# A two-layer hybrid decoder trunk on one core: earlier cache pages, 230 GB/s assumed for transfers, a hand-ordered second MLP and four branch steps moved to ScalarE

## The chip, the cores and the metric

The kernel runs on one core of one Trainium2 chip. The metric is the device time of one execution in microseconds (us). Engines are named as in the profile: PE is TensorE's matmul, PEld its weight load, DVE is VectorE, ACT is ScalarE, POOL is GpSimd, SP is SyncE, which here issues the DMA transfers.

## The reference, cut to what matters

Two layers, width 1024, over 1024 prompt rows and 8 samples of 4 rows each (1056 rows in all). Float32 throughout.

```python
# even layer: attention of 8 heads of 64 beside a recurrent branch of width 512
q, k, v, xr, g = jnp.split(u @ w_in, [512, 1024, 1536, 2048], axis=-1)
attn = _stick_breaking(q, concat(past_k, k), concat(past_v, v), sb_bias, q_offset)
xc   = bias + sum(w[j] * xp[:, j:j + t] for j in range(4))        # causal conv of xr
r, i = sigmoid(xc @ wa + ba), sigmoid(xc @ wx + bx)               # 8 blocks of 64
a    = exp(-8 * softplus(-lam) * r)
inp  = sqrt(-expm1(2 * log_a)) * (i * xc)
h    = scan(h = a * h + inp)
out  = concat(attn, gelu(g) * h) @ w_out
# odd layer: 16 heads, three dilated windows (128,1), (512,4), (2048,16), merged by their denominators
# behind each mixer:
h = h + square(relu(rms_norm(h) @ w_ff1)) @ w_ff2                 # 1024 -> 4096 -> 1024
```

For the samples, `past_k` and `past_v` are gathered from a pool of pages by a page table: 8 samples with 8 pages of 128 keys, so 64 pages of keys and 64 of values, 256 KB each.

## The kernel before, in words

**Matmuls.** Activations lie transposed, features on partitions and the 1056 rows in three pieces of 352 columns (`CW`). Float32 operands are split into a high and a low part, and a product is three matmuls (`mm3`). A raw weight tile `ws` is split by ScalarE, which copies the high part (two instructions of 128x512), and GpSimd, which subtracts it for the low part (one of 128x1024). One weight unit (128x1024) feeds 72 matmuls of 352 columns.

**Order of the work.** Two kinds of stretches follow each other. In most of them the tile framework's scheduler orders each engine. In the attention stretches and in the first MLP the order is written by the program: generators of attention steps, projections and sample steps are merged by `interleave`, and a small planner (`Clock`, L60, and `Timed`, L128) keeps for each engine and tile the time at which it expects it to be free. Deferred steps (`after`, L263, a delay in columns of 1/2.4 ns) come up when their time has passed. A transfer costs the planner its bytes at 360 GB/s (L143). Cache pages and other work tiles come from a ring of 18 tiles `u` and are handed back by `drop`; the planner picks the one that it expects free first.

**Stages of the even layer.**
- The recurrent branch: four blocks of 128 features. PE projects `xr` and `g`, DVE takes them out of PSUM (`xr<-mm,rstd`, `g<-mm,rstd`). `lru_conv` (L638) makes `xc` (a scaled copy of `xr`, then three shifted multiply-adds). `lru_block` (L658) makes the GELU factor `ge`, the gates `u` and `ig` (PE matmuls, ScalarE sigmoids), `a` and `z` by ScalarE's exp, tanh and reciprocal root, then on DVE `w = u + 1`, `e = (a+1)*w`, `e = 0.25*e - 1`, `e = (a+1)*e` and so on to the scan `hsc`. GpSimd multiplies `ge` and `ig`.
- Attention of four pairs of heads: `heads` and `projections` interleaved. The first three pairs run before the sample stage; the fourth is interleaved with it. Results go to DRAM (`mix<-o`) and come back transposed (`x<-mix`).
- The sample stage `sb_samples` (L1436): a generator that first asks for four pages (`fetch`), splits and places the queries, then takes 64 key pages and 64 value pages, four of them in flight, and asks for the next as each is used. It is created behind the loop over the pairs. Beside it runs `early_out`, the half of the output projection that the branch feeds.

**MLPs.** `finish_layer` (L1213) makes the output projection and norm, then the MLP: 8 groups of 4 up units (`w1`, 128 hidden features each) and 4 down units (`w2`, 256 outputs each). For layer 0 `first_mlp` (L1264) writes the order of all five engines by hand: the raw weight of unit `u+4` is asked for and that of unit `u+2` is cut in two halves between the pieces of unit `u`. For layer 1 a plain loop asks for each unit's weights in place and the scheduler orders it; the last four down units come from `last_weights`, and `last_pass` (L1367) does the last group together with the final norm, transposes and stores.

In the loop of layer 1 a hidden piece takes this path (L1242 to L1250):

```python
nc.vector.scalar_tensor_tensor(t, ps, 0.0, rstd[:, s], op0=OP.max, op1=OP.mult)
nc.scalar.activation(q, t, AF.Square)
nc.scalar.activation(th[f][:, s], q, AF.Copy)
nc.vector.tensor_sub(tl[f][:, s], q, f32(th[f][:, s]))
```

and a down unit adds its product to `h` on DVE (`h<-mm,h`). Up and down products share two PSUM tiles `mm`.

Of the kernel before, what the change touches and what calls it, by code (L numbers as in the profile page):

```python
# [11 lines left out]
F = mybir.dt.float32  # L12
# [24 lines left out]
def f32(ap):  # L37
    return ap.bitcast(F)
# [89 lines left out]
class Timed:  # L128
# [5 lines left out]
    def __getattr__(self, n):  # L134
        f = getattr(self.engine, n)

        def call(*args, **kw):
            r = f(*args, **kw)  # L138
            aps = [a for a in list(args) + list(kw.values()) if hasattr(a, "name") and hasattr(a, "shape")]
            outs = aps[:1] + ([kw["accum_out"]] if "accum_out" in kw else [])  # L140
            if self.e == "sync":
                o = aps[0] if aps[0].space != DRAM else aps[1]
                cost = int(np.prod(o.shape)) * 4 / 360 * 2.4  # L143
                outs = [a for a in outs if a.space != DRAM]
                ins = [a for a in aps[1:] if a.space != DRAM]
            else:
                a, b = Timed.NS[self.e]
                ins = aps[1:]
                c = int(np.prod(aps[0].shape[1:]))
                if self.e == "vector" and c >= 256:  # L150
                    big = [i for i in ins if i.space != PSUM and int(np.prod(i.shape[1:])) == c]
                    b *= 2 if "scan" in n else 1.6 if len(big) > 1 else 1
                cost = (a + b * c + (130 if "accum_out" in kw else 0)) * 2.4
            self.clock.run(self.e, cost, outs, ins)
            return r
        call.timed = True
        return call
# [18 lines left out]
class Trunk:  # L176
# [152 lines left out]
        self.nc.sync.dma_start(s, src)  # L329
        return s  # L330

    def parts_w(self, kb, cols, pool=None, bufs=4):
        return [(pool or self.wp).tile([128, kb, cols], R, name=self.nm("w"), tag="w", bufs=bufs) for _ in range(2)]

    def split_w(self, s, h, l):
        kb = h.shape[1]
# [301 lines left out]
    def lru_conv(self, f, xr, oc, T):  # L638
        nc = self.nc
        V = self.vec[:, f]  # L640
        cw = [V[:, 32 + j:33 + j] for j in range(4)]
        xrs = xr[:, SEQ:].rearrange("p (b t) -> p b t", t=4)
        xc = T("xc")
        nc.vector.tensor_scalar(xc, xr, cw[3], V[:, 36:37], op0=OP.mult, op1=OP.add)
        xp = T("xp", shape=(128, 8, 7))
        nc.gpsimd.tensor_copy(xp[:, :, 0:3], V[:, 0:24].rearrange("p (b j) -> p b j", j=3))
        nc.gpsimd.tensor_copy(xp[:, :, 3:7], xrs)
        xcs = xc[:, SEQ:].rearrange("p (b t) -> p b t", t=4)
        for j in (2, 1, 0):
            d = 3 - j  # L650
            nc.vector.scalar_tensor_tensor(xc[:, d:SEQ], xr[:, :SEQ - d], cw[j], xc[:, d:SEQ],
                                           op0=OP.mult, op1=OP.add)
            nc.vector.scalar_tensor_tensor(xcs, xp[:, :, j:j + 4], cw[j], xcs, op0=OP.mult, op1=OP.add)
        nc.gpsimd.tensor_copy(oc[:, f, 0:3], xr[:, SEQ - 3:SEQ])
        nc.gpsimd.tensor_copy(oc[:, f, 3:27].rearrange("p (b j) -> p b j", j=3), xrs[:, :, 1:4])
        return xc

    def lru_block(self, f, g, xc, bd, sp4, tiny, oc, T):  # L658
# [2 lines left out]

        ge = T("ge")
        nc.scalar.activation(ge, g, AF.Square)
        nc.vector.tensor_scalar(ge, ge, 0.044715, 1.0, op0=OP.mult, op1=OP.add)
        nc.gpsimd.tensor_mul(ge, ge, g)
        u, ig = T("u"), T("ig")
        for dst, m, bc in ((u, bd[f], 37), (ig, bd[4 + f], 38)):
# [11 lines left out]
        nc.scalar.activation(u, u, AF.Tanh, scale=sp4[:, 0, f:f + 1])  # L679
        nc.scalar.activation(z, u, AF.Abs_reciprocal_sqrt, bias=tiny)  # L680
        w, e = T("w"), T("e")
        nc.vector.tensor_scalar_add(w, u, 1.0)
        nc.vector.scalar_tensor_tensor(e, a, 1.0, w, op0=OP.add, op1=OP.mult)
        nc.vector.tensor_scalar(e, e, 0.25, -1.0, op0=OP.mult, op1=OP.add)
        nc.vector.scalar_tensor_tensor(e, a, 1.0, e, op0=OP.add, op1=OP.mult)
        nc.vector.tensor_mul(a, u, e)
        nc.scalar.activation(a, a, AF.Identity, scale=2.0, bias=1.0)
# [321 lines left out]
    def layer0(self, st, rstd):  # L1009
# [4 lines left out]
        with self.pool("smp0") as sp, self.pool("qkv0") as qkv:  # L1014
            def TS(tag, bufs=1, dtype=F, shape=(128, NT)):
                return sp.tile(list(shape), dtype, name=self.nm(tag), tag=tag, bufs=bufs)
# [5 lines left out]
            with self.pool("pair0") as pool:  # L1022
# [52 lines left out]
                def load_lru(k):  # L1075
# [5 lines left out]
                att = self.heads(pps, lambda p, pp, h, i: self.sb_scores(pp, T, h, 2 * p + h, i),  # L1081
                                 k_step, v_step, T, False, done, 2)
                proj = self.projections(st, rstd, win, 512, pps, T)
                self.low_queries(T)
                with self.manual():
                    self.interleave((proj, 1))
                    for p in range(4):
                        self.split_pair(pps[p], T, False)
                        if p == 0:
                            self.after(60000, self.states_out, oc, TS("ot", shape=(36, LRU)), need=[oc])  # L1090
                        if p < 3:
                            self.interleave((att, 106.6 if p else 85.8), (proj, 76))
                    sample = self.sb_samples(smp, pps[3], ats, T, x, load, lambda: first.append(
                        self.out_w(self.i["w_out_ab"][0], range(4), 0, 9000)))
                    early = self.early_out(0, self.i["w_out_ab"][0], ops, range(4, 8),
                                           load_lru, lambda k: True, ("q32", "k32"), pps[3], T)
                    self.interleave((att, 126), (sample, 340), (early, 95))
# [115 lines left out]
    def finish_layer(self, l, ops, wsrc, ks, w):  # L1213
# [7 lines left out]
        with self.pool(f"mlp{l}") as hp:  # L1221
# [7 lines left out]
            w1 = self.i["w_ff1"][l].rearrange("(k p) f -> p k f", p=128)  # L1229
            w2 = self.i["w_ff2"][l].rearrange("(f p) d -> p f d", p=128)  # L1230
            nx = {}
            if l == 0:
                self.first_mlp(st, rstd, w1, w2, h, nx)
                return nx
            for g in range(8):
                th = [hp.tile([128, NT], R, name=self.nm("th"), tag="th", bufs=6) for _ in range(4)]
                tl = [hp.tile([128, NT], R, name=self.nm("tl"), tag="tl", bufs=6) for _ in range(4)]
                for f in range(4):
                    c0 = (g * 4 + f) * 128
                    w = self.weights(w1[:, :, c0:c0 + 128], 8, 128)  # L1240
                    if g == 7 and f == 3:
                        last = self.last_weights(w2)  # L1242

                    def ev(ps, s, f=f):
                        t = hp.tile([128, CW], F, name=self.nm("t"), tag="t", bufs=3)
                        q = hp.tile([128, CW], F, name=self.nm("t2"), tag="t2", bufs=3)
                        nc.vector.scalar_tensor_tensor(t, ps, 0.0, rstd[:, s], op0=OP.max, op1=OP.mult)
                        nc.scalar.activation(q, t, AF.Square)
                        nc.scalar.activation(th[f][:, s], q, AF.Copy)
                        nc.vector.tensor_sub(tl[f][:, s], q, f32(th[f][:, s]))  # L1250
                    for _ in self.project(st, w, ev):
                        pass
                if g == 7:
                    self.last_pass(last, th, tl, h)
                    break
                for m2 in range(4):
                    w = self.weights(w2[:, g * 4:g * 4 + 4, m2 * 256:(m2 + 1) * 256], 4, 256)
                    for _ in self.contract(w, (2 * m2, 2 * m2 + 1), range(4), th, tl, h):
                        pass
        return nx  # L1260

    def first_mlp(self, st, rstd, w1, w2, h, nx):  # L1264
        nc, hp = self.nc, self.hp
        todo = self.caches(hp)
        raw, parts = {}, {}

        def load(u):
# [7 lines left out]
        def cut(u, half):  # L1277
            if u >= 64:
                return
            if half == 0:  # L1280
                parts[u] = self.parts_w(*raw[u].shape[1:], *((hp, 2) if u % 3 == 2 else ()))
            (a, b), kb = parts[u], raw[u].shape[1]
            c = slice(0, kb // 2) if half == 0 else slice(kb // 2, kb)
            nc.scalar.activation(a[:, c], raw[u][:, c], AF.Copy)
# [8 lines left out]
        cut(1, 0)  # L1293
        cut(1, 1)
        load(3)
        next(todo)
        with self.tc.manual_schedule(engines={getattr(mybir.EngineType, e) for e in
                                              ("PE", "SP", "Pool", "Activation", "DVE")}):
            for u in range(64):
                g, x = divmod(u, 8)  # L1300
                if u + 4 < 64:
                    load(u + 4)
# [5 lines left out]
                if x < 4:  # L1308
                    for c in range(3):
# [14 lines left out]
                        next(todo, None)  # L1324
                        if c < 2:
                            cut(u + 2, c)
                    continue
                step = self.norm_done(h, self.g[:, 1], nx) if g == 7 else None

# [16 lines left out]
                    pass  # L1346
            for _ in todo:
                pass
        self.norm_finish(nx)


    def last_weights(self, w2):
        nc, hp = self.nc, self.hp
        ws = []
        for j in range(4):
            src = w2[:, 28:32, j * 256:(j + 1) * 256]
            if j in (0, 3):
                ws.append(self.weights(src, 4, 256))
                continue
            s, a, b = (hp.tile([128, NT], d, name=self.nm("w"), tag=t, bufs=n)[:, :1024].rearrange(  # L1360
                "p (k f) -> p k f", k=4) for d, t, n in ((F, ("acc", "sq")[j - 1], j), (R, "th", 6), (R, "tl", 6)))
            nc.sync.dma_start(s, src)
            self.split_w(s, a, b)
            ws.append((a, b))
        return ws

    def last_pass(self, ws, th, tl, h):  # L1367
        nc = self.nc
# [67 lines left out]
    def sb_samples(self, smp, pp, ats, T, x, load, ahead):  # L1436
# [22 lines left out]

        for _ in range(4):  # L1460
            fetch()
        for t in pp["split_s"]:
            t.run()

# [614 lines left out]
```

## Time and profile before

| | us |
|---|---|
| median of 3 runs | 3019.85 (3018.76 to 3021.5) |
| the profiled execution | 3023.94 |
| its span in the trace | 3022.2 |
| PE busy in the span | 2873.6 (95%) |
| DVE busy | 1666.2 (55%) |
| ACT busy | 1222.1 (40%) |
| POOL busy | 952.6 (32%) |

The stages by the trace: branch 42 to 219 us, attention of three pairs 219 to 430, its end and the first pages 430 to 450, key pages 450 to 570, value pages 570 to 675, first MLP 738 to 1470, dilated attention 1470 to 2210 with the samples in its last part, second MLP 2262 to 2957, last pass to 3022. A "wait" row names an engine's matmul that had nothing to do, and what released it. The chain of waits is followed back from the last instruction; a row of it is a piece of the path that set the end. The granted clock is a share of TensorE's full 2.4 GHz.

### The profile page before, as it was taken

The numbers are of one execution on the slowest core, as the hardware profiler recorded it, in microseconds if no ns is written. First come the engines' busy times: TensorE is split into PE (matmuls) and PEld (weight loads), VectorE is DVE, ScalarE is ACT, GpSimd is POOL, SyncE is SP. The second block draws the span as 40 slices with busy tenths as digits, with TensorE's granted clock in tenths as the row PEclk, the third lists the DMA queues.
The fourth block names the chain that finished last, engine by engine and source line by source line (L and its number), as shares of the span: only waits on it lengthen the run. The fifth ranks groups of instructions, "written<-read, shape, count | busy, mean of one in ns | idle before, by whom it ended". The sixth has DMA issues, their size and how long they took to land.

```text
span 3022.2 us, 49205 instructions
## 1 busy us (share of the span) xinstructions
PE 2873.6 (95%) x18608; PEld 2730.8 (90%) x18608; DVE 1666.2 (55%) x3597; ACT 1222.1 (40%) x2441; POOL 952.6 (32%) x591
## 2 busy tenths in 40 slices
PE   7889889999999999999999999998989999999998
PEld 6778879659999999999999989997889999999998
DVE  5877897544444444442467878866663332333335
ACT  4455676434343333332455555544342221212222
POOL 2445562123333333341432222223132121212122
PEclk9999999999999999999999999999989999999999
DMA  5111136664877778861355656566531111111111
GB/s 174 43 50 30 43 106 224 191 211 138 253 247 246 252 252 254 258 222 40 131 185 161 216 160 212 158 221 195 169 128 43 49 43 49 43 49 43 50 36 65
DMA packets 366725, 426.16 MB, mean 141 GB/s; under 512 B 23878, under 2 KB 292822, under 8 KB 366488
## 3 DMA queue, kind: packets, MB, share of 16 engines
q1 hardware_dynamic: 366488, 423.01, 43.7%
q8 instruction: 147, 2.41, 0.3%
q14 instruction: 90, 0.74, 0.1%
HBM read 296.23 MB, written 126.17 MB: 140 GB/s over the span
## 4 chain that ended last, share of the span: by engine, by line
PE 73%; DVE 11%; DMA 4%; ACT 4%; issue 4%; POOL 1%; SPq 1%; ACTq 0%; POOLq 0%; DVEq 0%
PE mm L213 58%; PE tr L213 9%; PE tr L219 3%; PE pv L213 2%; DMA ws<-in_w_in_c_dram 1%; DVE u L138 1%; DVE sa L138 1%; DVE w L138 1%; DVE xl L138 1%; DVE f L138 1%; DVE sb L138 1%; ACT w L138 1%; ACT u L138 1%; DMA U<-kv 1%; DVE tl L138 1%
## 5 line engine op out<-in xcount | busy, mean ns | idle before, releaser
L213 PE MATMUL mm<-xh,w 128*128 128x352 f32 x5184 | 1337.0, 329 | 24.8 <-DVE xr L138 7.1
L213 PEld LDWEIGHTS mm<-xh,w 128*128 128x128 f32 x5184 | 926.7, 191 | 34.8 <-DVE xr L138 8.4
L138 POOL TENSOR_TENSOR w<-ws,w 128x1024 fp32r<-128x1024 f32 (+1 forms) x188 | 464.4, 2471 | 1290.1 <-ACT w L138 1194.5
L213 PE MATMUL mm<-xl,w 128*128 128x352 f32 x2592 | 844.8, 326 | 2.8 <-DVE xl L138 2.8
L213 PE MATMUL mm<-th,w 128*128 128x352 f32 (+2 forms) x3072 | 742.0, 323 | 6.1 <-DVE h L138 6.1
L213 PEld LDWEIGHTS mm<-th,w 128*128 128x128 f32 x3072 | 532.7, 188 | 8.9 <-DVE h L138 8.4
L213 PEld LDWEIGHTS mm<-xl,w 128*128 128x128 f32 x2592 | 495.7, 191 | 6.8 <-DVE xl L138 3.1
L213 PE MATMUL mm<-tl,w 128*128 128x352 f32 (+2 forms) x1536 | 493.3, 321 | 0.0
L138 ACT ACTIVATE w<-ws 128x512 fp32r<-128x512 f32 (+1 forms) x376 | 220.3, 616 | 560.1 <-issue 265.1
L138 DVE TENSOR_TENSOR h<-mm,h 128x352 f32<-128x352 f32 (+2 forms) x384 | 200.3, 523 | 417.4 <-PE mm L213 417.4
L213 PEld LDWEIGHTS mm<-tl,w 128*128 128x128 f32 x1536 | 288.6, 188 | 0.0
L138 ACT ACTIVATE u<-tr 128x512 fp32r<-128x512 f32 (+5 forms) x362 | 188.3, 530 | 189.0 <-PE tr L219 151.5
L138 ACT ACTIVATE t<-t 128x352 f32<-128x352 f32 x192 | 95.2, 496 | 412.4 <-DVE t L138 412.4
L138 DVE TENSOR_TENSOR tl<-t,th 128x352 fp32r<-128x352 f32 x192 | 151.3, 788 | 192.6 <-ACT th L138 192.6
L138 DVE SCALAR_TENSOR_TENSOR t<-mm,rstd 128x352 f32<-128x352 f32 x192 | 100.5, 523 | 281.8 <-PE mm L213 276.9
L138 DVE TENSOR_TENSOR u<-tr,u 128x512 fp32r<-128x512 f32 (+3 forms) x272 | 164.0, 612 | 76.2 <-ACT u L138 73.6
L138 POOL TENSOR_TENSOR kvs<-raw,kvs 128x512 fp32r<-128x512 f32 x80 | 103.0, 1295 | 132.7 <-ACT kvs L138 73.8
L213 PE MATMUL pv<-u,v 128*128 128x256 f32 (+1 forms) x736 | 134.3, 298 | 10.7 <-DVE u L138 10.4
L213 PE MATMUL mm<-x,w 128*128 128x352 f32 x720 | 139.8, 333 | 3.7 <-DVE k L138 2.7
L213 PEld LDWEIGHTS pv<-u,v 128*128 128x128 f32 x736 | 107.3, 197 | 21.4 <-DVE u L138 13.3
L213 PEld LDWEIGHTS mm<-x,w 128*128 128x128 f32 x720 | 117.0, 192 | 10.5 <-issue 4.2
L138 DVE TENSOR_TENSOR_SCAN f<-f,ms 128x128 f32<-128x128 f32 (+3 forms) x64 | 100.4, 1569 | 35.6 <-ACT f L138 35.3
(278 smaller groups left out, 3663.6 us busy)
## 6 DMA issues: line engine op xcount, KB each, us to landing
kv<-kvs SPq DMA_DIRECT2D x160, 512.0 KB
U<-kv SPq DMA_DIRECT2D x160, 512.0 KB
ws<-in_w_ff_dram SPq DMA_DIRECT2D x126, 512.0 KB
raw<-in_cache_dil_k_dram SPq DMA_DIRECT2D x320, 64.0 KB
u<-in_cache_sb_k_dram SPq DMA_DIRECT2D x64, 256.0 KB
u<-in_cache_sb_v_dram SPq DMA_DIRECT2D x64, 256.0 KB
raw<-in_cache_dil_v_dram SPq DMA_DIRECT2D x64, 256.0 KB
out_dram<-u SPq DMA_DIRECT2D x48, 256.0 KB
```

What stands on the lines that cost most here:

```text
L138: r = f(*args, **kw)
L213: self.nc.tensor.matmul(out, w, x, start=start, stop=stop)
L219: self.nc.tensor.transpose(out, x, ident)
```

## The change

Four edits.

1. The planner counts a transfer at 230 GB/s in place of 360.
2. Four steps of the branch, 16 instructions, go from DVE `tensor_scalar` to ScalarE `activation(Identity)`: `xc` in `lru_conv`, `ge`, `w` and the scaled `e` in `lru_block`.
3. The sample generator is made before the loop over the pairs and stops once behind its first four fetches; that first part is a deferred step of 145000 columns (60 us) set at the third pair.
4. `first_mlp` becomes `units` and serves both layers. For layer 1 it runs 60 units; the last four are cut and given to `last_pass`, two of them (62, 63) in tiles of their own (`wl`). `last_weights` goes.

```diff
-                cost = int(np.prod(o.shape)) * 4 / 360 * 2.4
+                cost = int(np.prod(o.shape)) * 4 / 230 * 2.4
...
-        nc.vector.tensor_scalar(xc, xr, cw[3], V[:, 36:37], op0=OP.mult, op1=OP.add)
+        nc.scalar.activation(xc, xr, AF.Identity, scale=cw[3], bias=V[:, 36:37])
...
-        nc.vector.tensor_scalar(ge, ge, 0.044715, 1.0, op0=OP.mult, op1=OP.add)
+        nc.scalar.activation(ge, ge, AF.Identity, scale=0.044715, bias=1.0)
...
-        nc.vector.tensor_scalar_add(w, u, 1.0)
+        nc.scalar.activation(w, u, AF.Identity, bias=1.0)
         nc.vector.scalar_tensor_tensor(e, a, 1.0, w, op0=OP.add, op1=OP.mult)
-        nc.vector.tensor_scalar(e, e, 0.25, -1.0, op0=OP.mult, op1=OP.add)
+        nc.scalar.activation(e, e, AF.Identity, scale=0.25, bias=-1.0)
...
+                sample = self.sb_samples(smp, pps[3], ats, T, x, load, lambda: first.append(
+                    self.out_w(self.i["w_out_ab"][0], range(4), 0, 9000)))
...
+                        if p == 2:
+                            pages = self.after(145000, next, sample)
                         if p < 3:
                             self.interleave((att, 106.6 if p else 85.8), (proj, 76))
-                    sample = self.sb_samples(smp, pps[3], ats, T, x, load, lambda: first.append(
-                        self.out_w(self.i["w_out_ab"][0], range(4), 0, 9000)))
+                    pages.run()
...
         for _ in range(4):
             fetch()
+        yield 0, 0
...
-            for g in range(8):
...
-                    w = self.weights(w1[:, :, c0:c0 + 128], 8, 128)
...
-                if g == 7:
-                    self.last_pass(last, th, tl, h)
-                    break
...
+            self.units(l, st, rstd, w1, w2, h, nx)
...
+                where = (hp, 4, "wl") if l and u > 61 else (hp, 2) if u % 3 == 2 else ()
+                parts[u] = self.parts_w(*raw[u].shape[1:], *where)
...
-            for u in range(64):
+            for u in range(60 if l else 64):
...
+                    if l and u == 59:
+                        for v in (62, 63):
+                            cut(v, 0)
+                            cut(v, 1)
...
+        if l:
+            self.last_pass([parts[u] for u in range(60, 64)], th, tl, h)
+        else:
+            self.norm_finish(nx)
```

**Where it moves instructions.** VectorE in the branch, second block (its `w`, `e`, `z`, `a` are 876, 877, 872, 871) and the `xr` of the third (900). Before:

```order
L138 TENSOR_TENSOR xr_900<-mm_909,rstd_290 128x352
L138 TENSOR_SCALAR w_876<-u_849 128x1056
L138 SCALAR_TENSOR_TENSOR e_877<-a_871,w_876 128x1056
L138 TENSOR_TENSOR xr_900<-mm_935,rstd_290 128x352
L138 TENSOR_SCALAR e_877<-e_877 128x1056
L138 TENSOR_TENSOR w_876<-u_849,z_872 128x1056
L138 SCALAR_TENSOR_TENSOR e_877<-a_871,e_877 128x1056
L138 TENSOR_TENSOR z_872<-w_876,z_872 128x1056
L138 TENSOR_TENSOR a_871<-u_849,e_877 128x1056
L138 SCALAR_TENSOR_TENSOR w_876<-z_872,w_876 128x1056
L138 TENSOR_TENSOR xr_900<-mm_961,rstd_290 128x352
```

and with the change:

```order
L138 TENSOR_TENSOR xr_900<-mm_909,rstd_290 128x352
L138 TENSOR_TENSOR xr_900<-mm_935,rstd_290 128x352
L138 SCALAR_TENSOR_TENSOR e_877<-a_871,w_876 128x1056
L138 TENSOR_TENSOR xr_900<-mm_961,rstd_290 128x352
L138 TENSOR_TENSOR w_876<-u_849,z_872 128x1056
L138 SCALAR_TENSOR_TENSOR e_877<-a_871,e_877 128x1056
L138 TENSOR_TENSOR z_872<-w_876,z_872 128x1056
```

The third evacuation of `xr` now stands behind the first `e`, where eight rows of the chain stood ahead of it.

SP at the first pages (`u<-in_cache_sb_k_dram` is a page, `mix<-o` a pair's attention on its way to DRAM, `x<-mix` its return). Before:

```order
L138 DMA mix_85<-o_3886 64x256
L138 DMA mix_85<-o_4017 64x256
L138 DMA mix_85<-o_4032 64x256
L1453 TENSOR_LOAD pt
L1453 ISA x8
L138 ISA
L138 DMA u_4106<-in_cache_sb_k_dram 128x512
```

and with the change:

```order
L138 DMA mix_85<-o_3874 64x256
L1422 TENSOR_LOAD pt
L1422 ISA x8
L138 ISA
L138 DMA u_4038<-in_cache_sb_k_dram 128x512
L138 ISA
L138 DMA u_4077<-in_cache_sb_k_dram 128x512
L138 ISA
L138 DMA u_4079<-in_cache_sb_k_dram 128x512
L138 ISA
L138 DMA u_4081<-in_cache_sb_k_dram 128x512
L138 DMA mix_85<-o_4009 64x256
```

The four pages are moved ahead of the last two stores of attention results.

ACT at the end of a group's up units in the second MLP (`t` the square, `th` its high part, `w<-ws` a weight's high part). Before:

```order
L138 ACTIVATE t_7318_30950<-t_30949 128x352
L138 ACTIVATE th_30581<-t_7318_30950 128x352
L138 ACTIVATE w_31079<-ws_31077 128x512 x2
L138 ACTIVATE t_7321_30981<-t_30980 128x352
L138 ACTIVATE th_30581<-t_7321_30981 128x352
L138 ACTIVATE w_31170<-ws_31168 128x512 x2
```

and with the change:

```order
L138 ACTIVATE th_30603<-t_7346_30934 128x352
L138 ACTIVATE w_30939<-ws_30706 128x512
L138 ACTIVATE t_7351_30968<-t_30967 128x352
L138 ACTIVATE th_30603<-t_7351_30968 128x352
L138 ACTIVATE w_30939<-ws_30706 128x512
L138 ACTIVATE t_7354_31001<-t_31000 128x352
L138 ACTIVATE th_30603<-t_7354_31001 128x352
L138 ACTIVATE w_31036<-ws_30806 128x512 x2
```

The weight cut before the last piece is one half where it was two, and belongs to a unit further ahead.

## Rows read from the trace of the kernel before

**Rows 1.** Windows: busy time of each engine in stretches, clock, DMA share.
```profile
core 0: us, PE busy (x) PEld busy (x) DVE busy (x) ACT busy (x) POOL busy (x), PEclk, DMA share, GB/s
42.00:219.00 177.00, 152.27 (x827) 142.74 (x826) 132.44 (x151) 72.43 (x94) 78.69 (x51) 0.93 0.18 57
430.00:450.00 20.00, 9.18 (x79) 8.46 (x78) 18.90 (x23) 12.95 (x23) 17.08 (x18) 0.74 0.93 308
570.00:675.00 105.00, 104.58 (x382) 43.82 (x381) 48.82 (x92) 32.41 (x64) 20.39 (x17) 1.00 0.65 208
```
**Rows 2.** Waits of PE, 42 to 215 us: total, times, longest.
```profile
PE mm L213 <- DVE xr L138: 7.1, 2, 3.7
PE mm L213 <- DVE k L138: 6.4, 2, 5.0
PE mm L213 <- DVE g L138: 4.2, 3, 3.0
```
**Rows 3.** Groups of DVE, 42 to 219 us: busy, mean ns, idle before.
```profile
L138 DVE TENSOR_SCALAR w<-u 128x1056 f32<-128x1056 f32 x4 | 6.8, 1688 | 11.7 <-ACT u L138 11.7
...
L138 DVE TENSOR_SCALAR ge<-ge 128x1056 f32<-128x1056 f32 x4 | 4.6, 1142 | 3.9 <-ACT ge L138 3.9
L138 DVE TENSOR_SCALAR xc<-xr,vec 128x1056 f32<-128x1056 f32 x4 | 3.3, 824 | 0.1
L138 DVE TENSOR_SCALAR e<-e 128x1056 f32<-128x1056 f32 x4 | 2.8, 701 | 0.0
```
**Rows 4.** Timeline of the branch: start, duration, engine.
```profile
96.21 2.51 POOL L138 TENSOR_TENSOR ge<-ge,g 128x1056 f32<-128x1056 f32 x1 [0.59 <-ACT ge L138]
...
97.23 2.05 DVE L138 TENSOR_SCALAR w<-u 128x1056 f32<-128x1056 f32 x1 [2.73 <-ACT u L138]
...
98.51 1.18 ACT L138 ACTIVATE z<-u,tiny 128x1056 f32<-128x1056 f32 x1
...
195.64 0.68 DVE L138 TENSOR_SCALAR w<-u 128x1056 f32<-128x1056 f32 x1
```
**Rows 5.** Groups of ACT, 42 to 219 us.
```profile
L138 ACT ACTIVATE a<-a 128x1056 f32<-128x1056 f32 x4 | 4.3, 1082 | 11.9 <-DVE a L138 11.9
```
**Rows 6.** Timeline at the first pages: SP's queue, PE, DVE.
```profile
398.26 29.44 SPq L138 DMA_DIRECT2D mix<-o  x5
430.40 2.13 SPq L138 DMA_DIRECT2D u<-in_cache_sb_k_dram  x4
...
442.22 1.09 PE L219 MATMUL tr<-ident,u 128*128 128x128 f32 x4 [7.63 <-DMA u<-in_cache_sb_k_dram]
...
441.20 0.19 DVE L138 CAST x<-qsl 64x48 fp32r<-64x48 f32 x1
...
441.43 2.48 DVE L138 TENSOR_TENSOR u<-tr,u 128x512 fp32r<-128x512 f32 x4
```
**Rows 7.** Chain of waits in the sample stage: page landings.
```profile
474.54 5.09 DMA u<-in_cache_sb_k_dram
...
569.78 4.17 DMA u<-in_cache_sb_v_dram
```
**Rows 8.** Waits of PE, 2000 to 2210 us.
```profile
PE tr L219 <- DVE mx L138: 8.0, 3, 5.3
PE tr L219 <- DVE tl L138: 5.6, 1, 5.6
```
**Rows 9.** Chain of waits in both MLPs: start, duration, matmuls in the piece.
```profile
737.65 730.41 PE mm L213 x4555
...
2399.35 88.47 PE mm L213 x551
2487.89 1.15 ACT w L138 x2
...
2492.44 88.43 PE mm L213 x551
```
**Rows 10.** Waits of PE, 2262 to 3022 us.
```profile
PE mm L213 <- DVE h L138: 4.7, 7, 0.9
```

More of the change, by code (lines that the diff above doesn't have):

```diff
@@ L330, in raw_w, with parts_w @@
         return s
-    def parts_w(self, kb, cols, pool=None, bufs=4):
-        return [(pool or self.wp).tile([128, kb, cols], R, name=self.nm("w"), tag="w", bufs=bufs) for _ in range(2)]
+    def parts_w(self, kb, cols, pool=None, bufs=4, tag="w"):
+        return [(pool or self.wp).tile([128, kb, cols], R, name=self.nm("w"), tag=tag, bufs=bufs) for _ in range(2)]
     def split_w(self, s, h, l):
@@ L1231, in finish_layer, with units @@
             nx = {}
-            if l == 0:
-                self.first_mlp(st, rstd, w1, w2, h, nx)
-                return nx
-            for g in range(8):
[L1236 to L1239, printed above, removed]
-                    w = self.weights(w1[:, :, c0:c0 + 128], 8, 128)
[L1241 to L1252, printed above, removed]
-                if g == 7:
-                    self.last_pass(last, th, tl, h)
-                    break
[L1256 to L1259, printed above, removed]
+            self.units(l, st, rstd, w1, w2, h, nx)
         return nx
-    def first_mlp(self, st, rstd, w1, w2, h, nx):
+    def units(self, l, st, rstd, w1, w2, h, nx):
         nc, hp = self.nc, self.hp
-        todo = self.caches(hp)
+        todo = iter(()) if l else self.caches(hp)
         raw, parts = {}, {}
@@ L1280, in cut @@
             if half == 0:
-                parts[u] = self.parts_w(*raw[u].shape[1:], *((hp, 2) if u % 3 == 2 else ()))
+                where = (hp, 4, "wl") if l and u > 61 else (hp, 2) if u % 3 == 2 else ()
+                parts[u] = self.parts_w(*raw[u].shape[1:], *where)
             (a, b), kb = parts[u], raw[u].shape[1]
@@ L1295, in first_mlp @@
         load(3)
-        next(todo)
+        next(todo, None)
         with self.tc.manual_schedule(engines={getattr(mybir.EngineType, e) for e in
                                               ("PE", "SP", "Pool", "Activation", "DVE")}):
-            for u in range(64):
+            for u in range(60 if l else 64):
                 g, x = divmod(u, 8)
@@ L1348, in first_mlp @@
                 pass
[L1349 to L1365, printed above, removed]
+        if l:
+            self.last_pass([parts[u] for u in range(60, 64)], th, tl, h)
+        else:
+            self.norm_finish(nx)
     def last_pass(self, ws, th, tl, h):
```

## The prediction

> **What bounds the kernel now.** I read the windows first, stage by stage, since PE's 95% is a mean over stages with different limits. In the branch PE is busy 152.3 of 177 us beside DVE's 132.4 and ACT's 72.4; at the first pages PE works 9.2 of 20 us at a mean granted clock of 0.74; in the value pages PE is full, 104.6 of 105 [rows 1]. Then the waits of PE name who ends them: in the branch DVE's evacuations `xr` (7.1 us) and `g` (4.2), and behind it `k` (6.4) [rows 2]; at the first pages a page's transfer, 7.63 us [rows 6]; in the dilated tail DVE's `mx` (8.0) and `tl` (5.6) [rows 8]. Last the chain of waits in the MLPs: the first runs 4555 matmuls without a break, the second breaks between groups, with 551 matmuls between two breaks [rows 9]. So PE bounds nearly all of it, and the change can gain only where PE waits. The sum below is made against the profiled execution, 3023.94 us; the median of the runs is 3019.85, 4.1 lower, and I carry the difference over.
>
> **Part 1: the second MLP, -5 us (-6 to -3).** The rows at 2399.35 and 2492.44 are one group apart: 93.09 us [rows 9]. Without a break a group of 8 units with 72 matmuls each has 576 matmuls, and the first MLP's 730.41 us for 4555 gives 0.16036 us each, so 92.37 us [rows 9]. The loss is 0.72 us a group. The waits agree in place: PE waits 7 times for DVE's `h`, 4.7 us in all [rows 10]. The cause stands in the chain: ACT cuts a weight, two instructions in 1.15 us, in front of the last hidden piece's square [rows 9]; the piece's low part comes late on DVE, `h` stands behind it, and both PSUM tiles are full. In the new order one half cut stands there and it belongs to a unit further ahead. The order is the first MLP's, whose stretch has no break. 7 x 0.72 = 5.0. The last group's two extra cuts run on ACT and POOL beside PE's four earlier units; if they delay the last pass, one cut's 1.15 us is the price, which makes the lower end of the gain.
>
> **Part 2: four steps on ScalarE, -5 us (-12 to +4).** From DVE go 16 instructions: 6.8 + 4.6 + 3.3 + 2.8 = 17.5 us [rows 3]. The mean of `w` hides two prices: 2.05 us at 97.23, where a GpSimd multiply runs from 96.21 to 98.72, and 0.68 alone at 195.64 [rows 4]. DVE's step waits here for GpSimd's to end, so when it leaves, part of that wait falls on the next step that meets GpSimd. At the undisturbed prices, for which I take the nearest rows 0.68 for `w` and `ge`, 0.82 for `xc` and 0.70 for `e`, a block gives back 2.88 us and four give 11.5. That is the lower end of what DVE is freed of, 17.5 the upper.
>
> The Trainium skill, page "SBUF — State Buffer", section "Who interferes with whom", says that a VectorE instruction in a two-port mode and GpSimd exclude each other for a whole instruction; the 2.05 beside 0.68 agrees, and by that rule alone the freed time would be all 17.5.
>
> To ACT come 16 instructions of about 1.08 us, the price of `a<-a` with the same size and function [rows 5]: 17.3 us on an engine that is busy 72.4 of 177 [rows 1]. On the path they cost something: `w` must now stand behind `z`, which ends at 99.69, so it ends near 100.8 where DVE ended it at 99.28 [rows 4], 1.5 us later a block; `e` goes to ACT and back, 1.08 for 0.70, plus up to one weight cut (1.15) ahead of it. But PE waits for evacuations, not for `w` or `e` [rows 2], and these move up: by the order excerpt the third `xr` stands behind the first `e` instead of behind eight rows of the chain. I take half of the 11.3 us of waits for `xr` and `g`, less some 1 us for later `w` and `e`: -5. The best end is all of 11.3 and a little; the worst is in the rivals.
>
> **Part 3: the first pages, -3 us (-7 to +1).** Now the first page is issued at 430.40, behind five stores of attention that SP sends from 398.26 on, and PE waits 7.63 us up to 442.22 [rows 6]. With the change it is asked for behind the third store; the five spread over 29.4 us, so that is near 413, some 15 us sooner. Not all 7.63 us go: the sample's queries are placed on DVE until 441.39 and the next DVE step starts at 441.43 [rows 6], so scores can't begin much sooner than today; what can go is the transposes and the catch-up behind them. I take 2.5 us and a little for the slow clock, 0.74 over these 20 us [rows 1]; the best end is nearly the whole wait. Against it: four of 18 work tiles are held 15 us longer, and a page that waits on SP for its tile holds up the two stores behind it. Their way back, `x<-mix`, has the rest of the key stretch as cover; if a tile is late by a DVE step the price is about 1 us.
>
> **Part 4: 230 for 360, -1 us (-12 to +12).** This is no operation; it shifts where `interleave` puts steps. In the sample stage the planner now spaces uses of a page wider apart and fills with the fourth pair's attention and `early_out`. The stretch has 105/64 = 1.64 us of PE work a value page with four pages in flight [rows 1], so pages are late only if a landing exceeds 4 x 1.64 = 6.6 us; landings in the chain are 5.09 and 4.17 [rows 7]. PE has 0.4 us idle there, so nothing can be won; pulling filler ahead may cost a little at the end: +1 (-4 to +6). In the dilated tail PE waits 8.0 and 5.6 us for DVE [rows 8]. The changed order puts some 60 matmuls of the output projection ahead of the last transposes where about 25 short ones stood; that may cover part: -2 (-10 to +6). The attention of the first three pairs I cost at nothing: DVE is its bound and its work is the same.
>
> **Sum.** -5 - 5 - 3 + 1 - 2 = -14. 3023.94 - 14 = 3010 for a run like the profiled one; 3019.85 - 14 = 3006 against the median.
>
> **Rivals.**
> - *The branch's chain moves to ScalarE: slower.* DVE already waits 11.7 us for ACT's `u` and ACT 11.9 for DVE's `a` [rows 3, 5]: the two hand the block back and forth. If that chain, not the evacuations, sets the end of the branch, each block pays 1.5 for `w`, 0.4 and 1.15 for `e`, 0.26 for `xc` and 0.4 for `ge`: 3.7, so 15 for four. Then -5 - 3 + 15 = +7, 3027. It decides when DVE has nothing else at the time `w` comes back. Against it: DVE is busy three quarters of the stretch, so there is mostly something to do.
> - *ScalarE, nothing won.* The freed DVE time and the longer chain cancel, and pages, landing early, still find DVE late: only the MLP's 5 us remain, 3015. The Trainium skill, page "ScalarE: Activation LUTs", section "Rules for kernel authors", says to keep plain additions and multiplications on VectorE. The rows agree on the price of a single step: 1.08 on ACT against 0.68 to 0.82 on an undisturbed DVE [rows 3 to 5].
> - *The tail of the dilated stage too.* If the waits for `mx` and `tl` go wholly, 13.6 us [rows 8] in place of the 2 assumed: 3006 - 12 = 2994.
> - *The rate makes pages late.* Past a landing of 6.6 us each further us costs 64/4 = 16 us. It needs landings 1.5 us above the longest row [rows 7]; I count it inside the slower case.
>
> **How the numbers follow.** A difference of 0.2%, 6.0 us, is about what a measurement of this kernel can tell: same lies from 3013.8 to 3025.9. Chances: the forecast 0.58 (its own range 2996 to 3013), nothing won in the branch and at the pages 0.20, the dilated tail too 0.12, slower 0.10. Faster is 0.58 + 0.12 = 0.70. The range from 2990 to 3023 leaves out the slower case and the best part of the tail case, and takes in the unknown sizes of parts 2 and 4 between.
>
> **What would show it.** In the profile after: no wait for `h` at group boundaries, and pieces of the chain 92.4 us a group; waits for `xr` and `g` under 7 us, and the branch ending some 5 us sooner; the first page landed before 432 and PE's wait there down from 7.6 to about 5; waits for `mx` and `tl` near 11. The forecast is wrong if ACT has idle time ended by DVE's `e` on the chain, if any page row of the sample stage exceeds 6.6 us, or if the dilated tail moves by more than 6 us.

## The result and the profile after

The changed kernel took 2999.59 us (median of 4 runs, 2994.2 to 3000.74) against 3020.26 us: a ratio of 0.9927, 95% interval 0.9915 to 0.9939, so some 21 to 22 us less (18 to 26). Forecast were 14. The profiled execution after is the quickest of its four, 2994.2 us with a span of 2992.4; the one before (3023.94) lies above its median. Their difference, 30 us, is therefore too large by about 9, and stages are read from several profiles below.

Windows of the kernel after, the stretches of [rows 1] (columns as there):

```profile
42.00:219.00 177.00, 150.73 (x848) 141.86 (x846) 114.64 (x133) 87.77 (x109) 73.49 (x50) 0.93 0.19 58
430.00:450.00 20.00, 13.74 (x121) 13.20 (x122) 17.07 (x23) 12.04 (x20) 17.88 (x17) 0.74 0.77 250
570.00:675.00 105.00, 105.00 (x381) 43.79 (x380) 43.46 (x87) 28.00 (x53) 18.63 (x12) 1.00 0.68 227
```

In the branch DVE lost 17.8 us of work (132.4 to 114.6) and ACT gained 15.3, yet PE is not busier. The waits of PE in the branch (42 to 215 us) say why. Two more of before, beside [rows 2]:

```profile
PE mm L213 <- DVE q L138: 3.9, 1, 3.9
PE tr L213 <- issue: 2.6, 1, 2.6
```

and after:

```profile
PE tr L213 <- issue: 7.7, 1, 7.7
PE mm L213 <- DVE q L138: 6.2, 1, 6.2
PE mm L213 <- DVE k L138: 4.4, 1, 4.4
PE mm L213 <- DVE g L138: 4.0, 3, 3.2
PE mm L213 <- DVE xr L138: 2.6, 1, 2.6
```

`xr` fell from 7.1 to 2.6 as the order promised, but the single wait marked "issue" grew from 2.6 to 7.7 and the one for `q` from 3.9 to 6.2. All waits of the window add up to 24.4 us before and 26.3 after. At the first pages and in the second MLP (waits 2236 to 2992 us, then the chain's longest piece) beside [rows 6, 9, 10]:

```profile
434.00 1.11 PE L219 MATMUL tr<-ident,u 128*128 128x128 f32 x4 [5.57 <-DVE u L138]
```

```profile
PE tr L219 <- DVE h L138: 1.0, 2, 0.5
PE pv L213 <- DVE y L138: 0.6, 1, 0.6
```

```profile
2235.49 692.63 PE mm L213 x4320
```

The wait at the first page is 5.6 us in place of 7.6, and the profile names DVE where [rows 6] names the page's transfer; e3 below shows that DVE ended it before the change too. The second MLP now has one piece of 4320 matmuls, all 60 units without a break, 0.1603 us each as in the first. In the dilated tail (waits 2000 to 2190 us), beside [rows 8]:

```profile
PE tr L219 <- DVE mx L138: 3.9, 3, 2.4
PE tr L213 <- DVE u L138: 2.1, 3, 1.6
PE tr L213 <- POOL w L138: 1.8, 1, 1.8
```

`tl` (5.6 us) has gone from the list and `mx` fell from 8.0 to 3.9.

### The profile page after: what moved, and what is told of

Same layout as the page of the kernel before. It is cut to its first block, busy times and chain, and to the rows that moved or that the text cites. A ratio compares the mean times of both kernels' runs of the same rounds, so it can differ in the third digit from the quotient of the medians.

```text
span 2992.4 us, 49203 instructions
## 1 busy us (share of the span) xinstructions
PE 2862.1 (96%) x18608; PEld 2722.4 (91%) x18608; DVE 1597.2 (53%) x3581; ACT 1236.3 (41%) x2456; POOL 946.8 (32%) x591
## 4 chain that ended last, share of the span: by engine, by line
PE 79%; DVE 10%; ACT 4%; issue 3%; DMA 2%; POOL 1%; SPq 0%; ACTq 0%; DVEq 0%; POOLq 0%
PE mm L213 63%; PE tr L213 10%; PE tr L219 4%; PE pv L213 2%; DVE u L138 1%; DVE sa L138 1%; DVE sb L138 1%; DVE f L138 1%; ACT u L138 1%; DVE xc L138 1%; DVE xl L138 0%; DVE w L138 0%; ACT w L138 0%; DMA u<-in_cache_sb_k_dram 0%; DMA ws<-in_w_out_c_dram 0%
## 5 line engine op out<-in xcount | busy, mean ns | idle before, releaser
L213 PE MATMUL mm<-xh,w 128*128 128x352 f32 x5184 | 1326.1, 328 | 17.8 <-DVE q L138 6.9
L213 PEld LDWEIGHTS mm<-xh,w 128*128 128x128 f32 x5184 | 922.1, 190 | 25.5 <-DVE q L138 7.5
L213 PE MATMUL mm<-xl,w 128*128 128x352 f32 x2592 | 841.9, 325 | 0.0
L213 PE MATMUL mm<-th,w 128*128 128x352 f32 (+2 forms) x3072 | 739.6, 323 | 0.0
L213 PEld LDWEIGHTS mm<-th,w 128*128 128x128 f32 x3072 | 532.4, 188 | 0.6
L213 PEld LDWEIGHTS mm<-xl,w 128*128 128x128 f32 x2592 | 494.3, 191 | 3.5 <-issue 0.2
L213 PE MATMUL mm<-tl,w 128*128 128x352 f32 (+2 forms) x1536 | 493.1, 321 | 0.0
L213 PEld LDWEIGHTS mm<-tl,w 128*128 128x128 f32 x1536 | 288.6, 188 | 0.0
L138 ACT ACTIVATE u<-tr 128x512 fp32r<-128x512 f32 (+6 forms) x362 | 188.5, 530 | 212.9 <-PE tr L219 193.7
L138 DVE TENSOR_TENSOR tl<-t,th 128x352 fp32r<-128x352 f32 x192 | 103.7, 540 | 181.7 <-ACT th L138 181.7
L213 PE MATMUL mm<-x,w 128*128 128x352 f32 x720 | 140.4, 335 | 4.9 <-DVE k L138 3.5
L213 PE MATMUL pv<-u,v 128*128 128x256 f32 (+1 forms) x736 | 133.0, 296 | 9.5 <-DVE u L138 8.8
L213 PEld LDWEIGHTS mm<-x,w 128*128 128x128 f32 x720 | 117.6, 192 | 16.8 <-issue 8.6
L213 PEld LDWEIGHTS pv<-u,v 128*128 128x128 f32 x736 | 104.2, 192 | 18.8 <-DVE u L138 11.3
```

Source lines behind the costliest of these rows:

```text
L213: self.nc.tensor.matmul(out, w, x, start=start, stop=stop)
```

## The experiments

Times as ratios to the kernel before, measured beside it on the same chip, 5 rounds each.

| run | what it has of the change | ratio | 95% interval | us |
|---|---|---|---|---|
| e1 | second MLP | 0.9983 | 0.9973 to 0.9992 | -5 |
| e2 | ScalarE steps | 1.0010 | 1.0001 to 1.0020 | +3 |
| e3 | early pages | 0.9981 | 0.9972 to 0.9990 | -6 |
| e4 | 230 | 0.9937 | 0.9924 to 0.9950 | -19 |
| e5 | all but ScalarE steps | 0.9928 | 0.9913 to 0.9944 | -22 |
| e6 | MLP and 230 | 0.9894 | 0.9877 to 0.9911 | -32 |
| e7 | 230 in the second layer alone | 0.9961 | 0.9947 to 0.9976 | -12 |
| e8 | as e5, with 150 | 1.0119 | 1.0099 to 1.0139 | +36 |
| e9 | all but early pages | 0.9914 | 0.9899 to 0.9929 | -26 |
| e10 | as e6, with 200 | 0.9981 | 0.9970 to 0.9992 | -6 |
| e11 | as e6, with 260 | 0.9978 | 0.9968 to 0.9988 | -7 |
| e12 | the whole change again | 0.9929 | 0.9916 to 0.9943 | -21 |

The last column is the ratio's distance from 1 times 3020.

**e1, the second MLP alone.** `first_mlp` becomes `units` for both layers as in the change; nothing else.

```diff
-            if l == 0:
-                self.first_mlp(st, rstd, w1, w2, h, nx)
-                return nx
-            for g in range(8):
+            self.units(l, st, rstd, w1, w2, h, nx)
```

> Only the second MLP's unit pipeline, the rest as before. Theory of the prediction: 7 breaks of 0.72 us go, -5 us (-6 to -3). Rival from the two traces, where the stretch from the layer-1 norm's start to the end of the hidden units shrank by 9: -8 to -9, because the norm ahead of the MLP is also passed sooner. If -2 or less, the breaks were replaced by something.

3015.3 us, -5 (-8 to -2). The chain has the same single piece (second row of this view of e1):

```profile
2252.85 2.29 PE tr L213 x18
2255.14 692.03 PE mm L213 x4320
```

The prediction's 5 lies in the middle of the interval, the rival's 8 to 9 at its edge. The traces speak for some 8. The matmuls of the down units, before and in e1:

```profile
L213 PE MATMUL mm<-th,w x1536: 288/322/428, 2301.4 to 3011.8; 128*128 128x352 f32 x168, 128*128 128x384 f32 x16, 128*128 128x288 f32 x8
L213 PE MATMUL mm<-th,w x1536: 288/322/428, 2298.8 to 3001.0; 128*128 128x352 f32 x168, 128*128 128x384 f32 x16, 128*128 128x288 f32 x8
```

From the first of them to the end of the span it is 720.8 us before and 712.6 in e1. The other profiles with the old order (e2, e3, e4, e7) have 720.3 to 720.6, all others with the new one 712.3 to 714.2. Of these 8 us some 6 lie ahead of the last group's down units; the last pass, counted from the last up matmul, is 1.5 us shorter (67.5 for 69.1), where the prediction feared a loss.

**e2, the ScalarE steps alone.**

```diff
-        nc.vector.tensor_scalar(xc, xr, cw[3], V[:, 36:37], op0=OP.mult, op1=OP.add)
+        nc.scalar.activation(xc, xr, AF.Identity, scale=cw[3], bias=V[:, 36:37])
-        nc.vector.tensor_scalar(ge, ge, 0.044715, 1.0, op0=OP.mult, op1=OP.add)
+        nc.scalar.activation(ge, ge, AF.Identity, scale=0.044715, bias=1.0)
-        nc.vector.tensor_scalar_add(w, u, 1.0)
+        nc.scalar.activation(w, u, AF.Identity, bias=1.0)
-        nc.vector.tensor_scalar(e, e, 0.25, -1.0, op0=OP.mult, op1=OP.add)
+        nc.scalar.activation(e, e, AF.Identity, scale=0.25, bias=-1.0)
```

> Only the four branch steps on ScalarE. Theory of the prediction: -5 us, third xr evacuation earlier. Rival A from the trace after, where the branch's last store moved by -2.1 and the first attention store by -0.3: -2 to 0, the gain is lost again before the first attention store. Rival B (ScalarE becomes the branch's chain): +5 to +15.

3023.68 us, +3 (0 to +6): not the gain of 5 forecast; rival A's 0 is the near end of the interval, rival B's +5 inside it. The profiled execution is the slowest of its 12 (3030.43); the wait read from it stands in the profile of the whole change too, 7.66 us. PE's timeline at the second and third blocks' gates:

```profile
108.74 1.94 PE L213 MATMUL tr<-xc,lru_wa 128*128 128x352 f32 x6
110.52 0.76 PE L213 MATMUL tr<-xc,lru_wx 128*128 128x352 f32 x2
112.81 1.45 PE L213 MATMUL tr<-xc,lru_wx 128*128 128x352 f32 x4 [1.54 <-ACT u L138]
121.93 2.69 PE L213 MATMUL tr<-xc,lru_wa 128*128 128x352 f32 x4 [7.67 <-issue]
```

and DVE's, where the third block's `xc` is finished:

```profile
118.31 2.34 DVE L138 TENSOR_TENSOR_SCAN hsc<-a,w 128x1056 f32<-128x1056 f32 x1
120.58 1.25 DVE L138 SCALAR_TENSOR_TENSOR xc<-xr,vec,xc 128x1021 f32<-128x1021 f32 x1
```

The same two in the kernel before:

```profile
120.78 2.68 PE L213 MATMUL tr<-xc,lru_wa 128*128 128x352 f32 x4 [2.59 <-issue]
119.41 1.27 DVE L138 SCALAR_TENSOR_TENSOR xc<-xr,vec,xc 128x1021 f32<-128x1021 f32 x1
```

PE came sooner to the third block's gates (its matmuls ahead of them end at 114.26, before at 118.19) and stood there 7.67 us, until DVE's last long multiply-add of `xc` ended at 121.83. The profile can name no releaser ("issue"), but in both kernels the gates start 0.1 us behind that step's end. `xc` was begun 7.4 us sooner (103.88 in place of 111.27) and finished 1.2 us later (121.83 in place of 120.68), since DVE still makes the second block's steps ahead of its multiply-adds. The wait moved from the evacuations of `xr` to the chain that follows them. DVE's groups show what GpSimd does to the steps that stayed (42 to 219 us), before:

```profile
L138 DVE SCALAR_TENSOR_TENSOR xc<-xp,vec,xc 128x32 f32<-128x32 f32 x12 | 9.3, 775 | 0.0
L138 DVE TENSOR_TENSOR a<-u,e 128x1056 f32<-128x1056 f32 x4 | 5.0, 1246 | 0.0
```

and in e2:

```profile
L138 DVE SCALAR_TENSOR_TENSOR xc<-xr,vec,xc 128x1023 f32<-128x1023 f32 (+2 forms) x12 | 18.9, 1575 | 4.7 <-ACT xc L138 4.7
L138 DVE TENSOR_TENSOR a<-u,e 128x1056 f32<-128x1056 f32 x4 | 11.7, 2913 | 0.0
L138 DVE SCALAR_TENSOR_TENSOR e<-a,w 128x1056 f32<-128x1056 f32 x4 | 5.8, 1462 | 6.4 <-ACT w L138 6.4
L138 DVE SCALAR_TENSOR_TENSOR xc<-xp,vec,xc 128x32 f32<-128x32 f32 x12 | 2.9, 239 | 0.0
```

`a<-u,e` had a mean of 1246 ns before and has 2913 now. Three of the four met a GpSimd step, one of them here:

```profile
133.77 3.48 POOL L138 TENSOR_TENSOR ge<-ge,g 128x1056 f32<-128x1056 f32 x1
134.85 3.52 DVE L138 TENSOR_TENSOR a<-u,e 128x1056 f32<-128x1056 f32 x1
```

But `xc<-xp` fell by 6.4 us. Over all groups of DVE steps that stand in the window in both kernels the sum is 121.3 us before and 119.7 in e2: the price of meeting GpSimd changed places, and did not eat up what the 16 steps gave back. DVE's waits for ACT fell as well, from 11.7 for `u` and 3.9 for `ge` [rows 3] to 6.4 for `w` and 4.7 for `xc`. DVE was freed as forecast; PE had no use for it.

**e3, the early pages alone** (the generator made ahead of the loop, its first part deferred; 360 kept).

```diff
+                        if p == 2:
+                            pages = self.after(145000, next, sample)
...
+                    pages.run()
```

> Only the earlier first pages, 360 GB/s kept. Theory of the prediction: -3 us (-7 to +1), PE's wait for the first page down from 7.6 to about 5. Rival: the wait for the first page goes and all of it is won, -7; other rival: pages land early and DVE is late, 0.

3015.44 us, -6 (-8 to -3), between the theory's 3 and the rival's 7. PE's longest wait is put down to DVE and is longer than forecast (waits 400 to 680 us):

```profile
PE tr L219 <- DVE u L138: 9.1, 1, 9.1
PE mm L213 <- DVE k L138: 2.9, 2, 2.7
```

DVE is late, as argued; but it was so before. In e1, whose first layer is that of the kernel before, the wait that [rows 6] puts down to the page's transfer is put down to DVE:

```profile
437.03 2.48 DVE L138 TENSOR_TENSOR u<-tr,u 128x512 fp32r<-128x512 f32 x4
437.82 1.09 PE L219 MATMUL tr<-ident,u 128*128 128x128 f32 x4 [7.67 <-DVE u L138]
```

In all four profiles with this code (before, e1, e2, e7) the matmul starts 0.79 us behind the start of DVE's step, in before at 442.22 behind 441.43 [rows 6], whichever releaser is named. So DVE's step set the end of the wait and not the transfer, and asking for it sooner did not shorten the wait here (with 230 it is 5.6 us with early pages, in the whole change and e5, and 7.1 without them, in e4 and e6). Nor does the profile show where the 6 us were won: from the first store of attention (`mix<-o`) to the first `h<-tr,h` behind the sample stage e3 takes 428.6 us, and before, e1 and e7, with the same code there, take 432.5, 429.3 and 430.7.

**e4, the rate alone.**

```diff
-                cost = int(np.prod(o.shape)) * 4 / 360 * 2.4
+                cost = int(np.prod(o.shape)) * 4 / 230 * 2.4
```

> Only 230 for 360 in the planner. Theory of the prediction: -1 us (sample stage +1, dilated tail -2). Rival from the trace after, where the dilated tail shrank by 13 us: -10 to -13, the waits for mx and tl go; the sample stage moves by less than 4.

3001.13 us, -19 (-23 to -15): by far the largest part, even above the rival, and outside the -12 to +12 of part 4. It divides in two. From the first `mix<-o` to the first `h<-tr,h` the profile takes 422.1 us, against the 429.3 to 432.5 of the three above. And the dilated stage takes 703.1 against 714.2. Over half of the first gain lies in the attention of the first three pairs, up to the request of the first page, which the prediction cost at nothing; before and e4:

```profile
244.80:430.00 185.20, 168.24 (x1101) 157.96 (x1101) 157.62 (x182) 119.39 (x250) 102.05 (x82) 0.98 0.14 37
244.30:424.60 180.30, 166.50 (x1092) 156.84 (x1091) 154.04 (x183) 119.70 (x250) 102.91 (x82) 0.98 0.14 38
```

It is 184.4 and 186.7 us in e1 and e7. PE is busier there than DVE, and DVE's busy time fell by 3.6 us with the order; what in the order did it was not traced.

**e7, the rate in the second layer alone.**

```diff
-                cost = int(np.prod(o.shape)) * 4 / 360 * 2.4
+                cost = int(np.prod(o.shape)) * 4 / self.clock.rate * 2.4
...
+            nc.rate = 230
             self.layer1(st, st["rstd"])
```

with `rate = 360` as the class's value. The file has one line more ahead of the helpers, so L214 there is L213 elsewhere.

> 230 only from the second layer on, 360 in the first; all else as before. Theory from the markers: about 12 of the 19 us of the rate lie in the dilated tail, so -11 to -13 here, the other -7 to -8 in the first layer's sample stage. Theory of the prediction: -2 here. Rival: the first layer carries most, -5 here.

3008.64 us, -12 (-16 to -7). The windows of the tail, cut at the last `tr<-U,qw` and the last `tr<-U,wst` of each kernel; before:

```profile
2114.10:2173.60 59.50, 53.94 (x395) 51.07 (x394) 34.55 (x131) 24.57 (x59) 10.66 (x8) 0.91 0.64 206
```

and e7:

```profile
2109.20:2157.00 47.80, 46.20 (x353) 43.32 (x353) 30.62 (x124) 20.49 (x51) 11.01 (x8) 1.00 0.54 175
```

PE idles 1.6 us in place of 5.6, and the mean granted clock of the stretch is 1.00 (2.4 GHz throughout) in place of 0.91: fewer waits, matmuls at the higher clock, and 42 matmuls fewer left for here. Over the whole dilated stage the number of matmuls is the same, before and in e7:

```profile
1487.50:2201.70 714.20, 680.65 (x4960) 640.34 (x4958) 522.85 (x1784) 357.92 (x855) 184.60 (x127) 0.98 0.57 183
1484.00:2185.60 701.60, 678.11 (x4961) 636.48 (x4959) 517.70 (x1785) 358.27 (x856) 182.45 (x127) 0.99 0.58 187
```

Of the 12.6 us 10.1 are waits and 2.5 are matmuls that take less time. PE's waits for `mx` fell from 14.1 to 6.4 us and those for `tl` from 5.6 to none; those for `u` rose from 3.4 to 6.8.

**e10 and e11, the rate on both sides of 230.**

```diff
-                cost = int(np.prod(o.shape)) * 4 / 230 * 2.4
+                cost = int(np.prod(o.shape)) * 4 / 200 * 2.4
```

and 260 in e11.

> Second MLP's pipeline alone, with 200 GB/s in the planner. If the gain comes from a broad optimum near the rate under load: within 6 us of the same kernel with 230 (2990). If 230 is a lucky order: 3000 or more.

> Second MLP's pipeline alone, with 260 GB/s in the planner. Broad optimum: within 6 us of the kernel with 230 (2990). Lucky order: 3000 or more; towards 360 it should approach 3015.

3014.92 and 3014.98 us: what the MLP alone gives. A lower rate as such wins nothing; 230 does. Two stretches bring it to the dilated stage: attention and samples from the first `mix<-o` to the first `h<-tr,h`, and the dilated stage from the first request of `U<-kv` to the last `sb<-sb,mx`:

| planner's rate | kernel | attention and samples, us | dilated stage, us | from, to |
|---|---|---|---|---|
| 360 | before | 432.5 | 714.2 | 1487.5 to 2201.7 |
| 360 | e1 | 429.3 | 716.1 | 1482.2 to 2198.3 |
| 360, then 230 | e7 | 430.7 | 701.6 | 1484.0 to 2185.6 |
| 230 | e4 | 422.1 | 703.1 | 1475.4 to 2178.5 |
| 230 | e6 | 425.1 | 701.2 | 1477.0 to 2178.2 |
| 200 | e10 | 418.8 | 726.3 | 1471.0 to 2197.3 |
| 260 | e11 | 424.5 | 726.5 | 1479.7 to 2206.2 |

The same stage's waits of PE, at 260:

```profile
PE tr L213 <- DVE mx L138: 19.4, 13, 3.5
PE tr L219 <- DVE mx L138: 8.1, 5, 2.9
PE tr L219 <- DVE sb L138: 6.3, 7, 1.1
```

At 230 `mx` comes to 6.4 in all (e7), before to 14.1. At 200 half of the loss against e7 is slower matmuls, 691.3 us at a mean granted clock of 0.96 for 4964 of them:

```profile
1471.00:2197.30 726.30, 691.28 (x4964) 647.52 (x4962) 508.81 (x1785) 358.34 (x856) 182.09 (x127) 0.96 0.55 180
```

In the first layer the lower rates do agree: 418.8 to 425.1 us against 429.3 to 432.5. At 200 and 260 the dilated stage takes this back. So the first layer's gain is broad, and the second layer's belongs, of the values tried, to one order; no value between 200 and 260 but 230 was tried, so how narrow it is stays open.

**e8, 150 GB/s** (as e5).

```diff
-                cost = int(np.prod(o.shape)) * 4 / 230 * 2.4
+                cost = int(np.prod(o.shape)) * 4 / 150 * 2.4
```

> As the run without ScalarE steps, but 150 GB/s in the planner. If a rate nearer to what transfers get under load is what helps, there is little more to win below 230: within 4 us of that run. If the shift of filler is what helps, more filler earlier helps on: faster by 4 or more. If the order at 230 was luck, it falls back to 3005 or more.

3054.42 us, +36. More filler earlier is not what helps: the last key page is asked for at 597.7, where e5 does so at 562.0, and the dilated stage grew to 735 us (701.8 in e5).

**e5, e6, e9, e12, how the parts combine.** e5 leaves out the diff of e2, e9 that of e3, e6 both; e12 is the changed kernel itself.

```diff
-        nc.scalar.activation(xc, xr, AF.Identity, scale=cw[3], bias=V[:, 36:37])
+        nc.vector.tensor_scalar(xc, xr, cw[3], V[:, 36:37], op0=OP.mult, op1=OP.add)
...
-                            pages = self.after(145000, next, sample)
```

> The whole change without the four ScalarE steps. Theory now: the steps cost, since alone they gave +4 us and the PE order puts the third block's gates ahead of ready data; so this is some 4 us faster than the whole change, 2995 to 2996. Theory of the prediction (the steps win 5): 3005.

> Only the second MLP's pipeline and 230, without early pages and ScalarE steps. Theory: with 230 the first pages are already asked for 6 us sooner and DVE is what PE waits for, so the early pages add nothing: within 2 us of the run without ScalarE steps, some 2996. Rival (parts add up: pages alone gave -4): 4 us slower than that run.

> The whole change without the early pages (230, second MLP's pipeline and the ScalarE steps stay). Theory now: with 230 the early pages cost some 8 us, since PE starts on the keys sooner and then waits for later pages and k between 450 and 510; the ScalarE steps cost 2 to 4. So 8 us faster than the whole change, 2992 (ratio to the kernel before near 0.990). Rival: what separated the two runs before was the order of that one kernel, and here the time equals the whole change within 3 us.

> The whole change again, beside the three others on one chip. Expected 0.9927 of the kernel before, 2999; waits in the sample stage as in its first profile (k 3.5 us, pages 1.7).

e5 at 3000.77 us equals the whole change: my expectation of 4 us less failed. e6 beat all: 2989.85 us, 10.9 below e5, measured beside it, and its interval (0.9877 to 0.9911) lies below that of the whole change in both measurements. e9 at 2994.83 us stands 4.6 below e12 (2999.44), measured beside it, with overlapping intervals, where I expected 8. So beside 230 the early pages cost: 11 us without the ScalarE steps, about 5 with them, although alone they won 6. The windows of the key stretch show a part of it; e5:

```profile
425.00:450.00 25.00, 17.16 (x153) 16.44 (x152) 22.79 (x29) 17.45 (x30) 20.63 (x20) 0.80 0.70 229
450.00:480.00 30.00, 26.79 (x260) 26.15 (x259) 17.54 (x29) 14.90 (x28) 2.37 (x1) 0.94 0.65 219
480.00:510.00 30.00, 25.75 (x247) 24.70 (x246) 19.49 (x33) 17.50 (x34) 5.14 (x6) 0.94 0.55 164
```

and e6, without early pages:

```profile
426.40:450.00 23.60, 13.85 (x104) 13.11 (x103) 21.19 (x26) 14.29 (x25) 18.92 (x18) 0.71 0.79 263
450.00:480.00 30.00, 29.14 (x284) 28.14 (x283) 19.94 (x31) 17.89 (x35) 5.83 (x5) 1.00 0.72 239
480.00:510.00 30.00, 28.58 (x269) 27.48 (x267) 22.81 (x34) 20.09 (x38) 10.23 (x9) 1.00 0.56 186
```

With early pages PE does 3.3 us more up to 450, and 5.2 less in the next 60, at a clock of 0.94: it waits for `k` (3.5 us) and pages (3.3), waits that e6 doesn't have. But e6 waits more for DVE's `u`, and all waits from 400 to 680 add up to 17.9 us in e5 and 15.7 in e6. From the first `mix<-o` to the first `h<-tr,h` e5 takes 431.9 us and e6 425.1, with 2680 matmuls each; of the 6.8 us 3.2 are idle time and 3.6 matmuls that take longer. The rest of the 10.9 lies in small differences behind it; the two MLP pieces make up 2 us of it (730.04 and 692.64 against 729.05 and 691.58, matmul for matmul). With the ScalarE steps the same stretch shows less: 425.8 and 426.7 us with early pages (the whole change, e12), 424.9 without (e9). So that they cost is shown by the times; by what wait, only in part.

## Why the prediction was right or wrong

The time fell inside the range, on the side forecast, and the difference was half as large again as the forecast. Its sum was right only in part, since two terms were mis-sized and cancelled partly, so it was partly luck: alone the rate gave -19 for -1 and the ScalarE steps +3 for -5. Of the signs that the prediction named, the waits for `h`, for `xr` and `g` (6.6) and at the first page (5.6) came as said. But `mix<-o` began 0.3 us sooner and not some 5, and the dilated tail moved by 12, which it had itself called a sign of being wrong.

- **Part 1, the second MLP, -5: right in place and cause, perhaps small in size.** Break by break, `h` is no longer waited for, the piece is 4320 matmuls long, and e1 gives -5 (-8 to -2). The traces show some 8 from the first down unit on: about 6 from the breaks, and 1.5 from a shorter last pass that had been put down as a risk. It was the one term in which both the present loss (93.09 against 92.37 us a group) and an example without it stood in the trace of before.
- **Part 2, ScalarE steps, -5: wrong in sign.** The step that failed is "I take half of the 11.3 us of waits for `xr` and `g`". The waits for `xr` did fall by 4.5 us. But the PE instruction behind them needs `xc`, the end of the same DVE chain, and PE stood there 7.7 us in place of 2.6, and 2.3 us longer for `q`: 26.3 us of waits in all for 24.4. The forecast counted DVE's freed time as if PE could use it wherever it arose. DVE did lose 17.8 us of busy time, the prediction's upper end. The rival "ScalarE becomes the branch's chain" has the sign, at a fifth of its price, but its mechanism is not shown: DVE waits less for ACT than before (11.1 us for 15.6), and ACT's new wait for `e` (5.5 us) is on no piece of the chain in the branch. For the branch "ScalarE, nothing won" came nearest.
- **Part 3, early pages, -3: the sign right alone, but not in company, and the loss misread.** The 7.63 us were no wait for a page's transfer: DVE's step ended them in the kernel before too, as e1 shows. The prediction saw that DVE bars the way until 441.39, and still took 2.5 us from that wait; in e3 the wait is 9.1 us, and the -6 lies elsewhere, where is open. What was missing besides is the rest of the key stretch: beside 230 the pages cost 5 to 11 us, of which waits for `k` and pages and slower matmuls at 450 to 510 are the part that was found.
- **Part 4, the rate, -1: mis-sized, and the main part of the result.** The dilated tail was given -2 of the 13.6 us of waits; it brought 12 (e7), as in the rival "the tail of the dilated stage too". The range (-10 to +6 for the tail) just missed it, and that of the whole part (-12 to +12) missed e4's -19. The attention of the first three pairs was put at nothing, since "DVE is its bound and its work is the same"; it took 180.3 to 182.5 us up to the first page's request with 200, 230 and 260 (e4, e6, e9, e10, e11), and 184.4 to 186.8 with 360 (before, e1, e7). The sample stage was given +1; none of these lower rates made it longer (236.4 to 244.4 us against 243.9 to 246.9). That one number of the planner has no size of its own was said ("this is no operation"), but not drawn into the middle value: e8, e10 and e11 lie at +36, -6 and -7. I found nothing in the old trace from which the size at 230 could have been read.
- **The sum.** Alone the parts give -5 + 3 - 6 - 19 = -27; together -21 to -22. The pages lose what they won. The second MLP and 230 together gave -32, 8 more than their sum; the intervals of e1, e4 and e6 leave room for that to be chance, and the 8 us of the MLP in the traces explain 3 of it.

**A version that beats both** is e6: second MLP and 230, without the early pages and without the ScalarE steps, 2989.85 us, 0.9894 of the kernel before. Whether 200 in the first layer (418.8 us there against 425.1) with 230 in the second would win more was not tried.

## What to carry to other kernels

A term is safe in place and sign when the trace holds both the loss and a stretch without it, as the two MLPs did. Before a wait is priced by the releaser that the profile names, see what else ended just ahead of it; a second profile of the same code can name another. Before time freed on one engine is booked as won, look up the next instruction of the engine that bounds, and what it needs: a shorter wait for the first tile of a chain turns into a wait for its last. Where a planner's constant orders the work, measure values on both sides: a gain at one value alone belongs to that order, need not survive the next edit, and need not add to other parts.

## What the runs showed that was not expected

Taking 17.5 us of steps off DVE moved its meetings with GpSimd to others: `a<-u,e` rose from 1246 to 2913 ns a piece without any change to it, and `xc<-xp` fell from 775 to 239. Waiting and a lower clock went together: in the dilated tail the granted clock was 0.91 with 5.6 us idle of 59.5, and 1.00 with 1.6 of 47.8, so part of what a removed wait gave back came from the matmuls beside it (2.5 of 12.6 us over the stage). And `xc` as an activation with scale and bias from columns took 1.26 us where `w`, with constants, took 1.07 for the same 128x1056 elements; why is not shown.
